# Layer 1's attention by groups of 32 queries: 176-key bands on eight parts of the array, square transposes on VectorE

## The chip, the cores and the metric

The kernel runs on one core of one Trainium2 chip. The metric is the device time of one execution in microseconds (us), the median of several. All tensors are float32 in memory; large products use two rounded halves of each operand (see below).

## The reference

A decoder trunk of two layers on 16 learned meta tokens and 256 tokens, 272 columns in all, width 2048. Layer 0 (gated linear attention, MLP) and the shared keys and values come before the place of the change; layer 1's MLP and the final norm come behind it. The change touches only layer 1's attention: 32 query heads of 64, 4 key and value heads, a sliding window of 128, the 16 meta tokens seen by all, and one learned sink per head in the softmax. Cut to that:

```python
q = rope((xn @ w_q).reshape(B, L, 32, 64), pos) * 64 ** -0.5
ok = meta (k < 16, k <= q)  or  band (k >= 16, 0 <= q - k < 128)
s = where(ok, einsum(q, keys), -1e30)
s = concatenate([s, sink])              # one column per head
p = softmax(s)[..., :-1]
o = einsum(p, vals)
h = h + o @ w_out
```

## The kernel before, in words

Activations lie transposed: 128 features on the partitions, tokens along the columns, 16 such tiles of the stream `h`. A weight comes in pieces of 128 x 1024 floats (512 KB): `fetch` (L83) issues the transfer on the SP queue into `raw` (four buffers), `split_weight` rounds it to `hi` on ScalarE (L91) and puts the rest in `lo` on VectorE (L93), three buffers each; VectorE's subtraction needs ScalarE's result. `passes` (L124 to L130) multiplies hi by x.hi, hi by x.lo, lo by x.hi: 24 matmuls for a piece of `w_q`, 256 columns each. A `product` is two pieces into one PSUM bank, after each of which it calls `after`.

Layer 1's attention runs interleaved with `w_q` and the first round of `w_out_b`. There are eight steps (class `Step`), each for four query heads: two products make its queries (`query`, four pieces, copied to `qt` at L908), and `rope` (L815 to L821) turns them into `QR`, with four copies by DMA on GpSimd's queue for the swapped halves `sw`. Behind each of the four pieces of step t there is a slot for attention work of earlier steps: in slot 0 the transposes of step t-4, in slot 2 the values of t-4 and both scores of t-2. Attention of one step is:

- `scores(0)` for 112 queries (plus 16 that are not used) against 128 keys, `scores(1)` for 128 queries against 256 keys, in PSUM banks `s` (L921);
- `soft` (L873): on VectorE, mask and sink added in and the row maximum taken, in one instruction per head, into `pr`;
- `normalise`: negated maximum (L882), exponential with row sum (L885) on ScalarE, sum and reciprocal (L887, L888) on VectorE, scaling of `pr` by the reciprocal: the 256-column part on VectorE (L891), the 128-column part on ScalarE (L893);
- `transposes` (L932): twelve 128 x 128 on TensorE, copied out by ScalarE as `PT` (L934);
- `values` (L943): six matmuls; the result is split into `O` by ScalarE (high part, L946) and VectorE (rest, L947).

The last 16 queries of all eight heads of a key head stand together in `qs` (copied by GpSimd, L912) and have their own `last_scores`, `last_transposes` and `last_values` (L953 to L980), once for every four steps. What is left of the last four steps runs behind products of `w_out_b` by the table `late`, whose keys are the product's number in round 0; each such product is one piece, and VectorE adds it to `h` at L172. PSUM has eight banks, four in pool `acc` for products and values, four in `aux`.

TensorE's order is that of the program text (`manual_schedule`); the order on the other engines is worked out by the framework's scheduler when the program is built, and each engine then takes its instructions in that order. So a wait at the head of VectorE's or ScalarE's queue holds up all behind it, `lo` and `hi` of the next pieces among them.

## Time and profile before

| | |
|---|---|
| three runs | 2042.64, 2042.83, 2045.62 us; median 2042.83 |
| the profiled execution | 2042.74 us, of which span 2041.0 |
| granted TensorE clock in it | 0.998 of full speed |
| busy in the span | TensorE 99%, VectorE 67%, ScalarE 53%, GpSimd 10% |
| layer 1's attention | about 1166 to 1310 us in the span |

In the page, PE is TensorE's matmuls, PEld its weight loads, DVE VectorE, ACT ScalarE, POOL GpSimd, SP the engine whose queue fetches the weights. A group row names source line, engine, operation, tiles (out<-in), shape and count, then busy time and the mean of one in ns, then the engine's idle time ahead of it and who ended it. Durations of neighbouring instructions overlap, since an engine is pipelined; what one costs in a row of its kind is the distance of starts, which the timeline gives. An fp32 matmul leaves two records.

### The profile page before, as it was taken

How to read it: one execution, taken by the hardware profiler on the slowest of the kernel's cores; microseconds unless marked ns; L12 is line 12 of the kernel's file. 1: busy time of each engine (PE TensorE's matmuls, PEld its weight loads, DVE VectorE, ACT ScalarE, POOL GpSimd, SP SyncE). 2: the span in 40 equal slices, each digit the busy share in tenths (PEclk: the TensorE clock that was granted, in tenths of full speed). 3: DMA queues.
4: the chain of work that ended last, by engine and by line, in shares of the span. 5: the costliest groups of instructions: out<-in, count | busy, mean ns of one | idle time of the engine just before them, and what ended most of it. 6: DMA issues, size and time to landing. Idle time of an engine off the chain costs nothing.

```text
span 2041.0 us, 39089 instructions
## 1 busy us (share of the span) xinstructions
PE 2022.1 (99%) x15978; PEld 1946.1 (95%) x15978; DVE 1374.7 (67%) x2035; ACT 1073.5 (53%) x1693; POOL 202.1 (10%) x209
## 2 busy tenths in 40 slices
PE   9999999999999999999999999999999999999997
PEld 9999999999999999999999999999999999999997
DVE  7799677665555555555566787796666666666666
ACT  6565665454345434534544577666436545545653
POOL 0000233400000000000023111160000000000032
PEclk9999999999999999999999999999999999999999
DMA  7644446565555555655554654466666666666662
GB/s 243 196 157 146 149 151 196 188 232 190 187 192 190 188 193 187 190 192 188 190 193 146 217 168 151 146 238 205 201 202 202 202 200 203 196 205 199 205 197 103
DMA packets 109124, 383.85 MB, mean 188 GB/s; under 512 B 13328, under 2 KB 15888, under 8 KB 108944
## 3 DMA queue, kind: packets, MB, share of 16 engines
q1 hardware_dynamic: 106640, 378.29, 57.5%
q8 instruction: 125, 2.05, 0.4%
q0 software_dynamic: 1152, 2.38, 0.4%
q10 hardware_dynamic: 1152, 0.68, 0.1%
q14 instruction: 55, 0.45, 0.1%
HBM read 376.82 MB, written 2.10 MB: 186 GB/s over the span
## 4 chain that ended last, share of the span: by engine, by line
PE 92%; DVE 3%; ACT 2%; issue 1%; POOL 1%; DMA 0%; SPq 0%; DVEq 0%; ACTq 0%; POOLq 0%
PE ps L124 23%; PE ps L128 18%; PE ps L130 18%; PE ps L129 18%; PE ps L125 12%; POOL sg L715 1%; DVE lo L93 1%; ACT hi L91 1%; PE ps L309 1%; PE s L921 0%; PE ps_pv L943 0%; PE pt L932 0%; ACT pr L885 0%; PE ps L311 0%; DMA raw<-in_w_in 0%
## 5 line engine op out<-in xcount | busy, mean ns | idle before, releaser
L93 DVE TENSOR_TENSOR lo<-raw,hi 128x1024 fp32r<-128x1024 f32 x707 | 871.7, 1234 | 476.4 <-ACT hi L91 470.3
L91 ACT CAST hi<-raw 128x1024 fp32r<-128x1024 f32 x707 | 738.8, 1046 | 826.2 <-PE ps L129 453.4
L130 PE MATMUL ps<-x,lo 128*128 128x272 f32 (+1 forms) x1904 | 531.8, 280 | 0.9 <-DVE lo L93 0.9
L128 PE MATMUL ps<-x,hi 128*128 128x272 f32 (+1 forms) x1904 | 531.6, 279 | 0.0
L129 PE MATMUL ps<-x,hi 128*128 128x272 f32 (+1 forms) x1904 | 531.1, 279 | 0.0
L130 PEld LDWEIGHTS ps<-x,lo 128*128 128x128 f32 x1904 | 359.9, 189 | 2.2 <-DVE lo L93 1.5
L128 PEld LDWEIGHTS ps<-x,hi 128*128 128x128 f32 x1904 | 360.2, 189 | 0.6 <-issue 0.4
L129 PEld LDWEIGHTS ps<-x,hi 128*128 128x128 f32 x1904 | 360.3, 189 | 0.1
L124 PE MATMUL ps<-x,hi 128*128 128x512 f32 x1024 | 335.7, 382 | 0.0
L124 PE MATMUL ps<-hid,hi 128*128 128x512 f32 x1008 | 330.1, 382 | 0.0
L128 PE MATMUL ps<-hid,hi 128*128 128x272 f32 (+1 forms) x1040 | 290.1, 279 | 0.0
L129 PE MATMUL ps<-hid,hi 128*128 128x272 f32 (+1 forms) x1040 | 290.1, 279 | 0.0
L130 PE MATMUL ps<-hid,lo 128*128 128x272 f32 (+1 forms) x1040 | 290.1, 279 | 0.0
L125 PE MATMUL ps<-x,lo 128*128 128x256 f32 x1024 | 279.1, 273 | 0.0
L125 PE MATMUL ps<-hid,lo 128*128 128x256 f32 x1008 | 274.1, 273 | 0.0
L124 PEld LDWEIGHTS ps<-x,hi 128*128 128x128 f32 x1024 | 193.5, 189 | 26.9
L124 PEld LDWEIGHTS ps<-hid,hi 128*128 128x128 f32 x1008 | 190.2, 189 | 26.4
L128 PEld LDWEIGHTS ps<-hid,hi 128*128 128x128 f32 x1040 | 196.6, 189 | 0.0
L125 PEld LDWEIGHTS ps<-x,lo 128*128 128x128 f32 x1024 | 196.6, 192 | 0.0
L129 PEld LDWEIGHTS ps<-hid,hi 128*128 128x128 f32 x1040 | 196.6, 189 | 0.0
L130 PEld LDWEIGHTS ps<-hid,lo 128*128 128x128 f32 x1040 | 196.6, 189 | 0.0
L125 PEld LDWEIGHTS ps<-hid,lo 128*128 128x128 f32 x1008 | 193.5, 192 | 0.2
(263 smaller groups left out, 2286.2 us busy)
## 6 DMA issues: line engine op xcount, KB each, us to landing
raw<-in_w_up SPq DMA_DIRECT2D x256, 512.0 KB, 4.3
raw<-in_w_down SPq DMA_DIRECT2D x256, 512.0 KB, 4.3
raw<-in_w_in SPq DMA_DIRECT2D x91, 512.0 KB, 3.4
raw<-in_w_out_a SPq DMA_DIRECT2D x32, 512.0 KB, 4.3
raw<-in_w_q SPq DMA_DIRECT2D x32, 512.0 KB, 4.3
raw<-in_w_out_b SPq DMA_DIRECT2D x32, 512.0 KB, 3.5
raw<-in_w_kv SPq DMA_DIRECT2D x8, 512.0 KB, 3.4
sw<-qt POOLq DMA_DIRECT2D x32, 64.0 KB, 3.5
```

Of the source, the lines that this page charges most:

```text
L91: nc.scalar.copy(hi, raw)
L93: splits.append(nc.vector.tensor_sub(lo, raw, hi.bitcast(F32)))
L124: nc.tensor.matmul(both, wh, x.both, start=begin, stop=False)
L125: newest[0] = nc.tensor.matmul(both[:, 1], wl, x.hi, start=False, stop=end)
L128: nc.tensor.matmul(out, wh, x.hi, start=begin, stop=False)
L129: nc.tensor.matmul(out, wh, x.lo, start=False, stop=False)
L130: newest[0] = nc.tensor.matmul(out, wl, x.hi, start=False, stop=end)
L309: nc.tensor.matmul(out, wk, xs[k].hi, start=False, stop=part == 1 and k == KT - 1)
L715: nc.gpsimd.tensor_scalar_max(sg, gt, -80.0)
```

## The change

The queries are now two parts of 128 (all 256 of the tokens behind the meta tokens), so the third part with `qs`, `m3`, `sinks3` and the `last_` functions is gone.

- Part 0 is scored against 144 columns (L933). Part 1 is scored in four groups of 32 queries, each against its own 176 keys: 16 meta and a band of 160 (L938). Its sixteen matmuls go round the eight 64-row by 32-column parts of the array. The bands stand in `KB`, copied once by GpSimd (L869, L870).
- `pr` holds the four heads of a part side by side with 16 columns of zeros behind each (L942), 640 or 768 columns. One instruction on VectorE transposes it in place in 32 x 32 squares (L906). No transpose of probabilities is left on TensorE, nor its copy on ScalarE.
- All scaling is on ScalarE (L904).
- `values` (L962) is 76 matmuls of 64 columns that go round the eight 32-row (some 16-row) by 64-column parts of the array and add up in four PSUM banks `pv`. The values stand for this as `VB`, 32 rows each, spread by 23 copies on the SP queue behind step 1 (L885 to L889).
- PSUM for this stage and the first round of `w_out_b`: two banks for products, two for scores, four for `pv`; afterwards four and four.
- The scores of part 0 stand in slot 0, those of part 1 in slot 2 behind the values, and `late` is new.

The diff, cut to what matters (`TILES` are the four slices of 32 partitions, `TW` is 32, `NM` 16):

```diff
+KEYS = (NM + P, 3 * NM + P)
...
+        def keys_of_blocks():
+            for g in range(1, len(TILES)):
+                nc.gpsimd.tensor_copy(KB[:, :, g - 1, :NM], KR[:, :, :NM])
+                nc.gpsimd.tensor_copy(KB[:, :, g - 1, NM:], KR[:, :, NM + g * TW:g * TW + KEYS[1]])
...
+        def spread_values():
+            for g, rows in enumerate(TILES):
+                for k, src in enumerate(TILES):
+                    nc.sync.dma_start(VB[rows, k:2 * len(TILES):len(TILES)], VT[src, :2])
+                if g:
+                    nc.sync.dma_start(VB[rows.start:rows.start + NM, NVB], VT[:NM, 0])
+                    nc.sync.dma_start(VB[rows.start + NM:rows.stop, NVB], VT[rows.start + NM:rows.stop, 0])
+            nc.sync.dma_start(VB[rows.start:rows.start + NM, NVB - 1], VT[:NM, 2])
...
-            for i, pr in enumerate(prs):
-                if pr.shape[-1] > P:
-                    nc.vector.tensor_scalar_mul(pr, pr, sm[:, i:i + 1])
-                else:
-                    nc.scalar.activation(pr, pr, AF.Copy, scale=sm[:, i:i + 1])
+            for c in range(4):
+                nc.scalar.activation(pr[:, c, :n], pr[:, c, :n], AF.Copy, scale=sm[:, c:c + 1])
+            flat = pr.rearrange("p c n -> p (c n)")
+            nc.vector.transpose(flat, flat)
...
+                    for g, rows in enumerate(TILES):
+                        for o, pp in zip(out, HALVES):
+                            keys = KB[pp, self.pair, g - 1] if g else KR[pp, self.pair, :n]
+                            nc.tensor.matmul(o[rows], self.QR[pp, i, P + g * TW:P + (g + 1) * TW], keys, start=True, stop=True)
...
             def values(self):
+                pv = pvp.tile([P, len(TILES), 512], F32, tag="pv", name="pv")
+                for part, pr in enumerate(self.probs):
+                    last = [g + 1 if part == 0 else 5 for g in range(len(TILES))]
+                    for k in range(6):
+                        for g, rows in enumerate(TILES):
+                            if k > last[g]:
+                                continue
...
+                            for par, kv in enumerate(HALVES):
...
+                                nc.tensor.matmul(dst, VB[tall, slot, self.pair, kv], src, start=k == 0, stop=k == last[g])
+                for part in range(2):
...
+                    nc.scalar.copy(oh, src)
+                    nc.vector.tensor_sub(ol, src, oh.bitcast(F32))
...
+        keys_of_blocks()
+        psum.close()
+        acc, aux, pvp = banks_of("acc2", 2), banks_of("aux2", 2), banks_of("pvp", 1)
...
+                if t >= 2:
+                    slots[0].append(partial(steps[t - 2].scores, 0))
+                    slots[2].append(partial(steps[t - 2].scores, 1))
+                if t >= 4:
+                    slots[2].insert(0, steps[t - 4].values)
...
+                if t == 1:
+                    spread_values()
...
+            late = {0: [partial(a6.scores, 0)], 2: [a4.values, partial(a6.scores, 1)], 4: [partial(a7.scores, 0)],
+                    6: [a5.values, partial(a7.scores, 1)], 9: [a6.values], 13: [a7.values]}
```

VectorE's order in one step of the steady part, before (L873 is the masking, L887 and L888 sum and reciprocal, L891 the scaling, L819 and L820 rope, L93 `lo`):

```order
L873 ISA mx 128x1
L883 TENSOR_TENSOR es<-sinks,mx 128x4
L887 TENSOR_TENSOR sm<-sm,es 128x4
L888 RECIPROCAL sm<-sm 128x4
L887 TENSOR_TENSOR sm<-sm,es 128x4
L888 RECIPROCAL sm<-sm 128x4
L891 TENSOR_SCALAR pr<-pr,sm 128x256 x4
L819 TENSOR_TENSOR QR<-qt,cos 128x512
L93 TENSOR_TENSOR lo<-raw,hi 128x1024 x3
L820 TENSOR_TENSOR sw<-sw,sin 128x2x256
```

Both parts' maskings end ahead of these rows, the two chains of sum, reciprocal and scaling follow each other, and three `lo` come in a row. After, from the end of the second part's masking (L944) to the first part's (L906 is the square transpose, L829 rope, L99 `lo`):

```order
L944 ISA mx 128x1
L897 TENSOR_TENSOR es<-sinks,mx 128x4
L901 TENSOR_TENSOR sm<-sm,es 128x4
L902 RECIPROCAL sm<-sm 128x4
L906 STREAM_TRANSPOSE pr<-pr 128x768
L99 TENSOR_TENSOR lo<-raw,hi 128x1024
L829 TENSOR_TENSOR QR<-qt,cos 128x512
L944 ISA pr,mx<-s,mask_14021,sinks 128x144
```

and from there to the second part's masking (L830 and L831 are rope, L967 the subtraction behind the values):

```order
L944 ISA mx 128x1
L99 TENSOR_TENSOR lo<-raw,hi 128x1024
L897 TENSOR_TENSOR es<-sinks,mx 128x4
L830 TENSOR_TENSOR sw<-sw,sin 128x2x256
L901 TENSOR_TENSOR sm<-sm,es 128x4
L831 TENSOR_TENSOR QR<-QR,sw 128x512
L902 RECIPROCAL sm<-sm 128x4
L99 TENSOR_TENSOR lo<-raw,hi 128x1024
L906 STREAM_TRANSPOSE pr<-pr 128x640
L99 TENSOR_TENSOR lo<-raw,hi 128x1024
L967 TENSOR_TENSOR O<-pv,O 128x4x64 x2
```

Each part's chain now stands alone between two maskings, with its square transpose ahead of a `lo`.

ScalarE's order in the same step, before (L882 negated maximum, L885 exponential, L893 scaling, L91 `hi`, L934 copy of `PT`):

```order
L882 ACTIVATE nm<-mx 128x4
L885 ACTIVATE pr,sm<-pr,nm 128x128 x4
L886 ACTIVATE es<-es 128x4
L882 ACTIVATE nm<-mx 128x4
L886 ACTIVATE es<-es 128x4
L885 ACTIVATE pr,sm<-pr,nm 128x256 x4
L893 ACTIVATE pr<-pr,sm 128x128 x4
L908 COPY qt<-ps 128x256
L91 CAST hi<-raw 128x1024 x2
L934 COPY PT<-pt 128x512 x3
L91 CAST hi<-raw 128x1024
```

and after (L896 negated maximum, L899 exponential, L904 scaling, L97 `hi`, L966 cast behind the values):

```order
L900 ACTIVATE es<-es 128x4
L899 ACTIVATE pr,sm<-pr,nm 128x176 x4
L904 ACTIVATE pr<-pr,sm 128x176 x4
L97 CAST hi<-raw 128x1024
L920 COPY qt<-ps 128x256
L97 CAST hi<-raw 128x1024
L896 ACTIVATE nm<-mx 128x4
L899 ACTIVATE pr,sm<-pr,nm 128x144 x4
L97 CAST hi<-raw 128x1024
L900 ACTIVATE es<-es 128x4
L97 CAST hi<-raw 128x1024
L904 ACTIVATE pr<-pr,sm 128x144 x4
```

The `hi` that followed the scaling of one part and stood beside the other part's work now stands behind a whole part's exponentials and scalings.

The SP queue held the 32 fetches of `w_q` in one row before. After, the 23 copies stand between the eighth and the ninth:

```order
L89 DMA raw<-in_w_q 128x1024 x8
L887 DMA VB<-VT 16x256
L885 DMA VB<-VT 32x2x256 x8
L888 DMA VB<-VT 16x256
L885 DMA VB<-VT 32x2x256 x4
L887 DMA VB<-VT 16x256
L888 DMA VB<-VT 16x256
L885 DMA VB<-VT 32x2x256 x4
L887 DMA VB<-VT 16x256
L888 DMA VB<-VT 16x256
L889 DMA VB<-VT 16x256
L89 DMA raw<-in_w_q 128x1024 x24
```

Each copy from the fourth on waits for a transfer that was issued eight before it, as the fetches do.

## The prediction

> **What bounds the kernel now.** I read the page first, then the attention stretch with the windows view, the groups by shape and the timeline. All times are us unless marked ns. Of the page, these lines:

> ```profile
> span 2041.0 us, 39089 instructions
> PE 2022.1 (99%) x15978; PEld 1946.1 (95%) x15978; DVE 1374.7 (67%) x2035; ACT 1073.5 (53%) x1693; POOL 202.1 (10%) x209
> ...
> PE 92%; DVE 3%; ACT 2%; issue 1%; POOL 1%; DMA 0%; SPq 0%; DVEq 0%; ACTq 0%; POOLq 0%
> ```

> TensorE is busy 99% of the span and carries 92% of the chain that ended last. The windows view of two stretches of layer 1's attention (columns: length, then PE, PEld, DVE, ACT and POOL busy, granted clock, DMA share, GB/s) shows how near the others are:

> ```profile
> 1192.00:1207.00 15.00, 15.00 (x137) 13.88 (x137) 14.06 (x44) 12.58 (x40) 3.37 (x5) 1.00 0.59 195
> 1237.00:1252.00 15.00, 14.71 (x136) 13.23 (x136) 11.68 (x34) 12.84 (x39) 3.26 (x5) 1.00 0.51 158
> ```

> PE has no gap to speak of, at clock 1.00. But VectorE is busy up to 14.06 of 15 us and ScalarE 12.6 to 12.8: if attention gets cheaper on PE, these two are next. The PE timeline gives the prices (start, length):

> ```profile
> 1166.63 0.28 PE L128 MATMUL ps<-x,hi 128*128 128x256 f32 x1
> ...
> 1194.05 0.28 PE L130 MATMUL ps<-x,lo 128*128 128x256 f32 x1
> 1194.17 1.47 PE L932 MATMUL pt<-ident,pr 128*128 128x128 f32 x12
> 1195.39 0.36 PE L128 MATMUL ps<-O,hi 128*128 128x256 f32 x1
> ...
> 1200.61 0.28 PE L129 MATMUL ps<-x,hi 128*128 128x256 f32 x1
> 1200.72 0.28 PE L130 MATMUL ps<-x,lo 128*128 128x256 f32 x1
> 1200.93 1.46 PE L943 MATMUL ps_pv<-PT,VT 128*64 128x224 f32 x12
> 1202.32 1.58 PE L921 MATMUL s<-KR,QR 64*128 64x128 f32 x16
> 1203.83 0.38 PE L128 MATMUL ps<-O,hi 128*128 128x256 f32 x1
> ...
> 1309.71 0.38 PE L128 MATMUL ps<-O,hi 128*128 128x256 f32 x1
> ```

> Product matmuls start 0.112 apart, so a piece (one 512 KB fetch, 24 matmuls) takes 2.68 and a step of four pieces 10.72. Transposes delay the next product matmul by 1.2 to 1.3 per step, values with both scores by 3.1 (1203.83 less 1200.72): a full step takes 15.1. From step 2's first matmul (1166.63) to the first after the last values (1309.71) lie 143.1; 24 + 14 pieces take 101.9 of it. So attention holds PE for 41.2 us. That is all the change can save there.

> **The change on PE.** Before shows nothing in 32-row parts; the nearest rows are small matmuls in column parts, early in the span:

> ```profile
> 120.44 0.38 PE L571 MATMUL ps_l<-W 128*32 128x32 f32 x18
> ...
> 141.43 0.22 PE L612 MATMUL ps_c<-QE,KD 128*64 128x64 f32 x1
> 141.44 0.22 PE L612 MATMUL ps_c<-KD,QE 128*64 128x64 f32 x1
> 141.49 0.22 PE L612 MATMUL ps_c<-QE,KD 128*64 128x64 f32 x1
> ```

> Two matmuls on different columns start 0.01 apart, the next pair (0.05 to 0.06, 0.058 over eight of them) later. Eight parts at once I take as the same, 0.058 per wave of 64 columns. Values are 76 fp32 matmuls of two records, 19 waves of one record for full eights, 22 with the uneven ends: 1.28, and 0.38 to change over when alone. First-part scores: four waves of 144 columns, 0.49 + 0.40 = 0.89. Second-part scores: four waves of 176 columns, 0.60, in one block with the values (0.55 of changeovers): 2.43. The sum is 8 x 0.89 + 2 x 1.0 + 6 x 2.43 + 2 x 1.66 = 27.0. All PE transposes and the 16-query third part are gone. If PE stayed the bound the change would win 41.2 - 27.0 = 14.2. If the eight parts ran one after another, a step's values would cost 76 x 0.058 = 4.4 instead of 1.28.
> [...]

> **The SP queue.** The 23 copies that spread the values stand between the eighth and ninth fetch of w_q. Rows of the fetches:

> ```profile
> L83 SPq DMA_DIRECT2D raw<-in_w_q x32: 327/328/335, 1132.7 to 1229.8; - x32
> ...
> DMA to landing us min/median/max: 3.1/4.3/5.9
> ```

> At 0.33 to 0.38 an issue they take 8.6; each also waits for the copy eight before it, two to three landings of 3 to 4. So the ninth fetch goes 9 to 10 us late. Four buffers of raw and those of hi and lo let a fetch lead its piece by some five pieces, 13.4; landing 4.3 and about 1.1 each for hi and lo leave 7 to 8 to spare (an estimate). PE waits 1.5 (0 to 4) at step 2.

> **VectorE and ScalarE.** Both work strictly in the order they are given, and this is what I expect to decide. Rows by shape (count, busy, mean ns, idle before), then the timeline:

> ```profile
> L93 DVE TENSOR_TENSOR lo<-raw,hi 128x1024 fp32r<-128x1024 f32 x48 | 58.3, 1223 | 16.6 <-ACT hi L91 16.4
> L172 DVE TENSOR_TENSOR h<-h,ps 128x256 f32<-128x256 f32 x16 | 6.6, 414 | 6.2 <-PE ps L130 6.2
> L820 DVE TENSOR_TENSOR sw<-sw,sin 128x512 f32<-128x512 f32 x8 | 5.5, 690 | 4.6 <-DMA sw<-qt 4.6
> L891 DVE TENSOR_SCALAR pr<-pr,sm 128x256 f32<-128x256 f32 x32 | 9.1, 350 | 0.3
> L908 ACT COPY qt<-ps 128x256 f32<-128x256 f32 x16 | 5.9, 366 | 0.0
> ```

> ```profile
> 1204.40 0.35 DVE L873 CUSTOM_DVE_ANT_0 pr<-s,m,sinks 128x128 f32<-128x128 f32 x1
> 1204.67 0.35 DVE L873 CUSTOM_DVE_ANT_0 pr<-s,m,sinks 128x128 f32<-128x128 f32 x1
> 1205.21 0.49 DVE L873 CUSTOM_DVE_ANT_0 pr<-s,m,sinks 128x256 f32<-128x256 f32 x1
> 1205.62 0.09 DVE L873 DVE_READ_ACCUMULATOR2_ANT mx<- 128x1 f32 x1
> ...
> 1209.57 0.16 DVE L887 TENSOR_TENSOR sm<-sm,es 128x4 f32<-128x4 f32 x1 [1.83 <-ACT pr L885]
> 1209.76 0.18 DVE L888 RECIPROCAL sm<-sm 128x4 f32<-128x4 f32 x1
> ```

> ```profile
> L885 ACT ACTIVATE pr<-pr,nm 128x128 f32<-128x128 f32 x32 | 12.5, 390 | 0.2
> ```

> ```profile
> 1208.46 0.49 ACT L885 ACTIVATE pr<-pr,nm 128x256 f32<-128x256 f32 x1
> 1208.95 0.49 ACT L885 ACTIVATE pr<-pr,nm 128x256 f32<-128x256 f32 x1
> ...
> 1209.44 1.26 ACT L893 ACTIVATE pr<-pr,sm 128x128 f32<-128x128 f32 x4
> 1210.61 0.35 ACT L908 COPY qt<-ps 128x256 f32<-128x256 f32 x1
> 1210.86 1.04 ACT L91 CAST hi<-raw 128x1024 fp32r<-128x1024 f32 x1
> ```

> Maskings start 0.27 apart for 128 columns and 0.41 for 256, so I take 0.285 for 144 and 0.32 for 176; exponentials 0.49 apart for 256 columns, some 0.10 less for 128 (mean 390 ns), so 0.41 and 0.43; scales (1210.61 less 1209.44, over 4) 0.29, so 0.31 and 0.33. A lo takes 1.18, a hi 0.95. For the square transpose no row exists: 0.35 for 256 columns (L891) gives 0.65 for 640 as the low end, twice lo's rate 1.5 as the high; nearest is lo's own rate, one element per step: 0.73 and 0.86.
> In before both maskings stand back to back and the exponentials of one run beside those of the other; even so VectorE waited 1.83 for the last exponential. In after each part is a chain of its own, with only one lo or none to fill it. From the second masking (S): maskings to 1.4, negated maximum and four exponentials to 3.5, sum and reciprocal 3.9, four scales 5.3, square transpose 6.2, lo, whose hi stands behind the scales, 6.35 to 7.5, cosine product 8.15. Then the first-part masking: maskings and a lo to 2.35, sw and sum 3.4, QR and reciprocal 4.3, lo to 5.5, square transpose (scales end at 5.65) 6.4, lo behind its late hi 6.7 to 7.85, then subtract, cast, subtract (0.41 like L172, 0.37 like L908), one after another because the second cast waits for the first subtraction: 9.05. Together 17.2. The last qt is copied only at S + 6.3, and its rope copies land thus:

> ```profile
> L817 POOL DMA_DIRECT2D sw<-qt x32: 536/536/553, 1157.6 to 1261.2; - x32
> ...
> DMA to landing us min/median/max: 1.8/3.8/5.9
> ```

> Four issues of 0.54 and a landing of 3.8 put sw at about S + 12.1, where VectorE asks for it at 10.65 (in before it waited 4.6 in all for these): 0 to 1.5 more, I take 0.8. The loop is then 18.0 per step, against PE's own 10.72 + 0.89 + 2.43 = 14.04, and against 15.1 before. PE would wait some 4 us in each step, at the third piece, for the lo behind the second transpose.

> **The sum.** Step 2 starts at 1168.1 (1166.63 + 1.5); two steps of 12.6 put step 4 at 1193.3 and its first masking at 1197.4. There three los, three square transposes and a wait for scales stand before the second masking: 11.6, so S is 1209.0. Four loops (17.6, the first less exposed to sw, then 3 x 18.0) and one without rope but with residual additions (16.3) give 1296.9. The lo of product 10 is done 7.4 later, and products 10 to 13 with the last values (1.66) take 12.4: 1316.7 against 1309.7. So 7 us slower: 2042.74 (this profiled run; its span 2041.0 and 1.74 around it) + 7 = 2049.7. The median of the three runs, 2042.83, is within 0.1. The rest of the kernel, two banks fewer for products in this stage aside (0 to 1 us), keeps its work. By the same sum loops of 16.6 give no change, 2043, and loops of 19 2055.

> **Rivals.**
> 1. PE stays the bound. If square transposes, exponentials and scales run faster than I take them, or the waits overlap, loops stay under 14.04 and the change wins 14.2 less the SP stall of 1.5: 2030. For it: PE carries 92% of the chain. Against it: 1.83 of waiting on one exponential already, in the looser order. Loops of 15 give about 2035. It decides where the loop passes 14.04.
> 2. Square transposes at twice lo's rate: +1.6 a loop over five loops, 2058.
> 3. The eight parts run one after another: the values cost 3.1 more per step on PE, 14.04 becomes 17.2, still under 18: the loop hides it and only the last two values show, +6: 2056.
> 4. The clock. In every row quoted it is 1.00, because PE never pauses; waits of 4 us are new. If one halves the clock for the next piece, 2.7 more lies on PE per step, of which slack takes half: some +7, 2057. [...]
> 5. The copies on SP land in time and the loop is a mere 16.6: no change, 2043. That the order is not followed by the chip is excluded: each engine's rows in the trace stand in program order.

> **How the numbers follow.** About 4.1 us (0.2%) is what a measurement of this kernel can tell from no change. Loop-bound near 2050: 0.45; loop about 16.6 and no change: 0.2; PE the bound or nearly (2030 to 2038): 0.25; transposes, parts or clock: 0.1. Slower takes 0.4 of the first and the 0.1, same 0.22, faster 0.28. The range 2033 to 2057 leaves out the lower half of the PE-bound case and the worst end; the loop's own range is 2043 to 2055.

> **What would show it.** Right: steps 4 to 7 about 18 apart, PE idle 3 to 5 us a step before a piece whose lo stands behind the 768-column transpose, VectorE idle on ScalarE's pr in each part. Wrong: PE without gaps and steps of 14; a square transpose far from 0.73 or 0.86; values far from 1.3; a stall elsewhere, as at the ninth fetch of w_q.

## The result and the profile after

The changed kernel takes 2077.56 us (median of four runs, 2077.15 to 2079.46), the kernel before 2042.74 beside it. The ratio is 1.0169, with a 95% interval of 1.0151 to 1.0187: 34.8 us slower, where 7 was forecast and 2057 was the top of the range. The sign was right, the size was not. The profiled executions stand 34.6 apart (spans 2075.6 and 2041.0).

The page of the changed kernel, its span, the engines and the chain that ended last:

```profile
span 2075.6 us, 41504 instructions
PE 2024.7 (98%) x17150; PEld 1947.5 (94%) x17150; DVE 1372.9 (66%) x2001; ACT 1069.5 (52%) x1683; POOL 200.9 (10%) x224
...
PE 84%; DVE 6%; ACT 4%; issue 2%; DMA 2%; POOL 1%; SPq 0%; DVEq 0%; ACTq 0%; POOLq 0%
```

TensorE's share of the chain falls from 92% to 84%. VectorE and ScalarE gain 5 points between them, and "DMA" and "issue", which the chain before hardly held, gain 3. Stretches of the windows view (columns as before: length, PE, PEld, DVE, ACT, POOL, clock, DMA share, GB/s):

```profile
1165.00:1180.00 15.00, 8.47 (x60) 7.99 (x60) 3.98 (x5) 3.51 (x4) 2.11 (x4) 0.77 0.72 216
1238.00:1258.50 20.50, 17.19 (x307) 15.94 (x306) 12.42 (x34) 11.81 (x36) 2.42 (x6) 1.00 0.38 107
1258.50:1277.40 18.90, 15.50 (x286) 13.77 (x284) 12.35 (x35) 11.82 (x36) 2.41 (x6) 1.00 0.42 127
```

The first is the ninth fetch of `w_q`: TensorE works 8.47 of 15 us and the mean granted clock is 0.77. The other two are one step each. PE now has gaps of some 3.4 us in each (3 to 5 were forecast), yet VectorE and ScalarE are busy only 12 of 19 to 20: no engine is full. The chain of waits in the first of those steps shows why (start, length, what; from second masking to second masking, 20.4 us):

```profile
1238.22 0.31 DVE pr L944
...
1239.94 1.71 ACT pr L899 x8
...
1242.49 1.09 ACT pr L904 x3
1243.58 0.93 ACT hi L97
1244.52 0.28 ACT qt L920
...
1245.08 1.42 POOL sw L827 x3
...
1246.66 5.47 DMA sw<-qt
...
1252.26 0.69 DVE sw L830
...
1254.18 1.02 ACT pr L904 x3
1255.20 0.94 ACT hi L97
...
1256.16 1.23 DVE lo L99
1257.39 0.34 DVE O L967
...
1258.16 0.42 DVE O L967
1258.59 0.31 DVE pr L944
```

TensorE does not occur in it. This is the loop of VectorE and ScalarE that the prediction drew, link for link, up to the subtraction of the second half of `O`. Its largest link is the landing of the rope copies, 5.47.

TensorE's own waits between 1160 and 1400 (waiting instruction, what ended the wait, total, times, longest):

```profile
PE ps L134 <- ACT qt L920: 8.1, 4, 4.5
PE ps L134 <- ACT hi L97: 6.1, 1, 6.1
PE ps L135 <- issue: 4.4, 3, 1.9
PE s L938 <- issue: 3.5, 2, 1.8
PE ps L130 <- DVE h L178: 2.5, 1, 2.5
PE pv L962 <- issue: 1.7, 1, 1.7
PE ps L136 <- DVE lo L99: 1.5, 3, 0.5
```

Four kinds: the loop (`qt`, 8.1: a product waits for one of its two banks until `qt` has been copied out), the SP queue (`hi`, 6.1), pauses that nothing in the profile releases ("issue", 9.6 in these rows), and one wait at the start of the last MLP (`h`, 2.5).

From the profiled executions the 34.6 add up so: 2.4 before step 2 (in it a gap of 1.04 that waits for a `lo`, and one of 0.90 behind the first change of PSUM pools); 8.6 at the ninth fetch; 18.5 from there to product 14; 5.1 behind it (a pause of 1.82, the MLP's gap of 2.80, and 0.5). Forecast were 0, 1.5, 5.5 and 0.

### The profile page after: what moved, and what is told of

It reads as the page before. It is cut to its first block, busy times and chain, and to the rows that moved or that the text cites. A ratio compares the mean times of both kernels' runs of the same rounds, so it can differ in the third digit from the quotient of the medians.

```text
span 2075.6 us, 41504 instructions
## 1 busy us (share of the span) xinstructions
PE 2024.7 (98%) x17150; PEld 1947.5 (94%) x17150; DVE 1372.9 (66%) x2001; ACT 1069.5 (52%) x1683; POOL 200.9 (10%) x224
## 4 chain that ended last, share of the span: by engine, by line
PE 84%; DVE 6%; ACT 4%; issue 2%; DMA 2%; POOL 1%; SPq 0%; DVEq 0%; ACTq 0%; POOLq 0%
PE ps L130 21%; PE ps L134 17%; PE ps L136 17%; PE ps L135 17%; PE ps L131 11%; DVE lo L99 2%; ACT hi L97 1%; POOL sg L721 1%; ACT pr L899 1%; ACT pr L904 1%; DMA raw<-in_w_in 1%; DMA sw<-qt 1%; DVE pr L944 1%; DVE x L189 1%; PE ps L315 0%
## 5 line engine op out<-in xcount | busy, mean ns | idle before, releaser
L99 DVE TENSOR_TENSOR lo<-raw,hi 128x1024 fp32r<-128x1024 f32 x707 | 871.5, 1233 | 483.1 <-ACT hi L97 476.7
L97 ACT CAST hi<-raw 128x1024 fp32r<-128x1024 f32 x707 | 738.4, 1045 | 828.7 <-PE ps L135 449.9
L134 PEld LDWEIGHTS ps<-x,hi 128*128 128x128 f32 x1904 | 360.9, 190 | 11.6 <-ACT hi L97 6.3
L130 PE MATMUL ps<-x,hi 128*128 128x512 f32 x1024 | 335.8, 382 | 2.5 <-DVE h L178 2.5
L130 PE MATMUL ps<-hid,hi 128*128 128x512 f32 x1008 | 330.1, 382 | 0.0
L130 PEld LDWEIGHTS ps<-x,hi 128*128 128x128 f32 x1024 | 193.5, 189 | 29.8 <-issue 2.8
L130 PEld LDWEIGHTS ps<-hid,hi 128*128 128x128 f32 x1008 | 190.2, 189 | 26.3
```

Source lines behind the costliest of these rows:

```text
L97: nc.scalar.copy(hi, raw)
L99: splits.append(nc.vector.tensor_sub(lo, raw, hi.bitcast(F32)))
L130: nc.tensor.matmul(both, wh, x.both, start=begin, stop=False)
L134: nc.tensor.matmul(out, wh, x.hi, start=begin, stop=False)
```

## The experiments

Theory A: the order loop sets the steps, as predicted, and the rest is the SP queue. Theory B: the two halves of the values and TensorE's pauses set them. Theory C, formed from the trace: four independent delays (loop, SP, code supply, change of pools) that partly cover each other. Each run has its ratio to the kernel before, timed beside it. "Steps" are the distances between second-part maskings in the three loops that the prediction put at 18.0 (the fourth to the sixth of seven); in the changed kernel they are 20.4, 18.8 and 19.3.

**1. The copies apart.** Two copies behind each piece of steps 1 to 3, instead of 23 in a row.

```diff
-                    nc.sync.dma_start(VB[rows, k:2 * len(TILES):len(TILES)], VT[src, :2])
+                    yield nc.sync.dma_start(VB[rows, k:2 * len(TILES):len(TILES)], VT[src, :2])
...
+                    for _ in range(2 if t else 0):
+                        next(spreading, None)
```

> The 23 copies that spread the values are issued two behind each piece of steps 1 to 3 instead of all behind step 1. In the changed kernel TensorE stands still from 1168.9 to 1175.3 for the ninth fetch of w_q and works the piece off until 1180.3, 8.7 us late, part of it at a granted clock of 0.77. If the SP queue did that and nothing later hides it: the pause shrinks to under 2, the clock in that stretch is 1.00, and the time falls by 6 to 8, to about 2070. If the loop of VectorE and ScalarE in steps 4 to 8 sets the end whatever comes before: no change, 2077.

2073.54 us, ratio 1.0145 (1.0129 to 1.016). The wait for `hi` goes and step 2's first scores start at 1171.57 instead of 1180.33. Of these 8.8 us only 4 reach the median. The profiled execution is the fastest of the four (2067.78; the others took 2073.25 to 2074.99) and keeps all of it: it ends 9.5 before that of the changed kernel. Where the others lose it is not shown.

**2. The values in two.** The first part's values behind the second piece, the second part's behind the third, each with its cast and subtraction.

> Values in two bursts, the first part's 28 matmuls behind the second piece of a step and the second part's 48 behind the third; same matmuls, same copies. Theory of code supply: the pauses of 1.2 to 2.1 on TensorE that nothing in the profile ends come because a burst of 76 fp32 matmuls is about 304 instructions in 1.9 us while a 16 KB packet on the instruction queue holds 256; bursts of 112 and 192 with a piece between them fit, so the pauses go and the time falls by 6 to 10, to about 2069. Theory of the order loop alone: the pauses in steps 4 to 8 are hidden in it, the time falls by at most 3 or so for the earlier cast of the first part, and pauses of about 2 stay.

2075.31, 1.0159 (1.0143 to 1.0174). The pauses named "issue" fall from 9.8 to 0.5, but a new wait takes their place, in the same banks of `pv`:

```profile
PE pv L964 <- DVE O L969: 14.4, 7, 4.0
```

The 256 instructions of the expectation are an estimate from pages of this case; the numbers stand under "Code supply" below.

**3. Both casts ahead of both subtractions.**

```diff
-                    nc.vector.tensor_sub(ol, src, oh.bitcast(F32))
+                    halves.append((ol, src, oh))
+                for ol, src, oh in halves:
+                    nc.vector.tensor_sub(ol, src, oh.bitcast(F32))
```

> Both casts behind the values first, then both subtractions, instead of cast, subtraction, cast, subtraction. Theory of the order loop: the last link ahead of the second masking gets 0.4 to 0.8 shorter in each of five loops, so the time falls by 2 to 4. Theory of code supply: nothing on TensorE changes, no change within 0.5.

2077.65, 1.017 (1.0155 to 1.0185): nothing is won in all. In the profiled execution, though, five of the seven loops are 0.1 to 0.8 shorter, and from the first second-part masking to the last it takes 121.6 instead of 123.5. But it has 27.3 us at half clock (a granted clock of 0.50) against 17.1, worth 5.1 at most. So the link was worth some 1.9, and the clock took it back.

**4. No square transposes.**

```diff
-            flat = pr.rearrange("p c n -> p (c n)")
-            nc.vector.transpose(flat, flat)
```

> Leaves out the square transposes on VectorE, so the probabilities go into the values untransposed. Theory of the order loop: 0.85 and 0.98 and the waits for the scalings ahead of them fall out of each loop; the distance of first-part maskings falls from 18 to 20 to about 16, the time by 8 to 14. Theory of code supply and of the SP queue alone: TensorE's pauses stay, the time falls by less than 2.

2076.18, 1.0171 (1.0154 to 1.0188). A miss: two transposes of 0.84 and 0.98 a step go, and the steps stay at 18.9 to 20.5. The two loops ahead of them are shorter (15.6 and 15.7 instead of 18.3 and 17.3); the last masking comes 3.6 earlier, and 1.5 of it reaches the end of the profiled execution. The `lo` behind a transpose waits for a `hi` that stands behind the same scales. The prediction's own times, 6.2 for one and 6.35 for the other, said so.

**5. Values in two bursts, both casts behind the second.**

> Values in two bursts of 28 and 48 matmuls with a piece of product between them, as in the run of two bursts before, but both casts and subtractions behind the second burst, as in the changed kernel. That run had lost its pauses without a releaser (11 us down to 0.5) and got 14.4 of waiting for the first part's subtraction in their place, because both parts share the four banks. Theory of code supply: without that wait the time falls by 8 to 12, to about 2067, and TensorE shows no pause of over 0.5 that nothing ends. Theory of the order loop: first-part maskings stay 18 to 20 apart in steps 5 to 8, and only the pauses behind the last values (some 6) are won: about 2071.

2074.39, 1.0146 (1.0131 to 1.0161). No "issue" wait is left, steps are 18.6 to 20.8. So the pauses were not what held the steps.

**6. Runs 1 and 5 together.**

> Two bursts with casts behind the second, and the 23 copies two behind each piece of steps 1 to 3. If SP queue, code supply and the half clock behind their pauses are separate costs, they add: 8.7 and 8 to 12 off, about 2057 to 2060. If the order loop of VectorE and ScalarE sets steps 5 to 8, the steps stay at 18 and the time is about 2063 to 2066.

2064.68, 1.0098 (1.0083 to 1.0113). Apart they win 4.0 and 3.2, together 12.9 (by the ratios 4.9, 4.7 and 14.5): each delay had covered part of the other. Some of it is clock: the mean granted clock is 0.995 here and 0.993 in runs 1 and 5, worth some 4.5 us at most.

**7. Run 6 without square transposes.**

> The same with the square transposes left out, so the probabilities go into the values untransposed. Theory of the order loop: now that TensorE has no pauses of its own the loop must show: first-part maskings come 1.5 to 2 closer, the time falls by 7 to 10 against the run with the squares. If VectorE's order is not what binds: the same within 2.

2062.93, 1.0091 (1.0074 to 1.0108): 1.75 less, not 7 to 10. It confirms run 4.

**8. The kernel before, with bursts of small matmuls.** 76 unused fp32 matmuls of 16 columns in steps 4 and 5, 38 in steps 6 and 7.

```diff
+                for k in range(n):
+                    kv = HALVES[k % 2]
+                    nc.tensor.matmul(pt[kv, :16], VT[0][:, 0, kv], KR[:, 0, :16], start=True, stop=True)
```

> The kernel before with a burst of unused small matmuls behind the second piece: 76 fp32 matmuls of 16 columns in steps 4 and 5, 38 in steps 6 and 7 (they go into a bank that nobody reads). Theory of code supply: each burst of 76 (304 instructions, more than a 16 KB packet of 256) shows a pause of 1.5 to 2.2 on TensorE in it or just behind it that nothing in the profile ends; the bursts of 38 (152 instructions) show none or under 0.5. Rival, that the pauses belong to the 32-row parts or to the banks: no pause with either.

A single execution: 2062.57, span 2060.9. The timeline around the first burst, and the window with it:

```profile
1199.43 5.07 PE L954 MATMUL pb<-KR,VT 128*64 128x16 f32 x152
1204.43 0.58 PE L128 MATMUL ps<-x,hi 128*128 128x256 f32 x1
```

```profile
1199.00:1210.00 11.00, 11.00 (x183) 10.62 (x183) 4.61 (x8) 4.38 (x11) 1.14 (x1) 0.70 0.46 153
```

It does not decide on code supply: on two parts the 152 records take 5.0 us (1199.43 to 1204.43), not the 1.98 of the values, so the burst is much less dense than that of the values, and no gap over 0.45 appears. Most of the 19.9 (2060.9 less 2041.0) are the bursts (5.0, 4.5 and twice 2.3) and 10.2 us at half clock, worth 5.1 at most. The granted clock fell to 0.70 in the window above without a pause; more on this below.

**9. The sum later.** Run 6, and the sum of the exponentials (L901) is ordered behind the next part's masking.

```diff
+                tc.add_manual_dep(getattr(waiting[-1], 'ins', waiting[-1]), getattr(masking, 'ins', masking).name, order, reason='order')
```

> Two bursts and copies apart as before (2064.7), and one ordering edge more per part: the sum behind the exponentials may stand on VectorE only behind the next part's masking. No instruction is added. Theory of the order loop (masking, exponentials, scales, hi, lo, masking, without TensorE): the chain of one part then runs beside the next part's, VectorE's waits of 12 us for exponentials go, first-part maskings come 16 instead of 19 apart, and the time falls by 8 to 14, to 2051 to 2057. Rival, that ScalarE's or TensorE's own work fills the steps: no change, 2064.

2062.1, 1.0088 (1.0073 to 1.0103); steps 17.6 to 18.2. VectorE's waits for exponentials go (`sm`, 12.1 in run 6). Those of the square transposes for the scales stay (12.8, now 13.2), and waits for the rope landing (4.3, now 9.1) and for `hi` (2.5, now 7.5) take their place.

**10. The square transposes later too**, behind the masking after the next.

> The same, and each square transpose behind the masking after next, so that it does not wait for the scales of its own part. Order loop: another 2 to 5 off, steps of 14.5 to 15.5, 2047 to 2053. Rival, as above: no change; or, if ScalarE's own 12 to 13 us a step now binds, no gain over the run before.

2057.96, 1.0067 (1.0051 to 1.0084); steps 17.0 to 18.5. VectorE's waits between 1190 and 1310 are now above all these:

```profile
DVE lo L99 <- ACT hi L97: 20.6, 11, 3.2
DVE sw L830 <- DMA sw<-qt: 6.5, 4, 3.0
```

**11. The two orders alone**, in the changed kernel.

> The changed kernel with the two ordering edges alone: values in one burst, copies in one block. Theory that costs of TensorE (code supply, half clock) and the order loop cover each other: the loop goes, the pauses of about 2 a step come onto the path, steps of 16 to 17, the time falls by 6 to 12, to about 2068. Rival, that the order loop alone sets steps 5 to 8: steps near 14.5, about 2060.

2071.38, 1.0133 (1.0118 to 1.0148). Steps fall to 16.7 to 18.1, but "issue" (8.8) and the stall at the ninth fetch remain. 6.2 us are won, as 6.7 were from run 6 to run 10.

**12. The rope product later.** Run 10, and `sw` times `sin` (L830) behind the next step's second masking.

> The kernel of e10_squares_later (copies apart, values in two bursts, exponential sums and square transposes behind the next masking), and the multiplication sw by sin (L830) is put behind the second masking of the next step as well, so that the second masking no longer stands behind the landing of the rope copies. In e10 VectorE waited 10.2 us in all for these landings. Theory (the order loop passes through the rope landing): steps fall from 17.0-18.6 to 15.5-16.5, the time from 2058 to 2049-2052. Rival A (the loop is held by ScalarE alone: hi behind exponentials and scales): the wait moves to lo<-hi, steps stay at 17-18, 2055-2058. Rival B (half-clock stretches hold the time): no change.

2051.24, 1.0038 (1.0024 to 1.0052), steps 16.9 to 18.0. Two steps of it:

```profile
1214.90:1231.80 16.90, 16.19 (x330) 14.71 (x329) 11.87 (x34) 11.74 (x36) 2.41 (x7) 1.00 0.48 143
1231.80:1248.70 16.90, 14.92 (x304) 13.96 (x294) 11.87 (x34) 11.74 (x36) 2.41 (x7) 1.00 0.48 143
```

6.7 us less: the rope landing was a link of the loop. Up to 3 us of it may be clock (on average 0.995 was granted in run 10, 0.997 here). With the link gone most steps are equal, 16.9, and VectorE waits mainly for `hi` (25.2 between 1190 and 1310, in 20 waits).

**13. Run 12 without scales.** The probabilities stay undivided.

```diff
-            for c in range(4):
-                nc.scalar.activation(pr[:, c, :n], pr[:, c, :n], AF.Copy, scale=sm[:, c:c + 1])
```

> As e12_swaps_later, but the four scales of every part are left out (the probabilities stay without their division by the sum). ScalarE loses eight instructions of 0.29 to 0.33 a step, 2.5 us. If ScalarE's queue is what holds the steps behind the edges, they fall by 2 to 2.5 more, to TensorE's own 14 to 15, and the time by 8 to 12 against e12, to 2040-2046. If the chain from exponentials to sum does not pass ScalarE's scales, 0 to -3.

2041.5, 0.9988 (0.9978 to 0.9998). A step:

```profile
1216.40:1231.30 14.90, 14.90 (x291) 13.98 (x290) 11.89 (x35) 9.28 (x28) 2.44 (x7) 1.00 0.59 163
```

TensorE is full, at 14.9 a step (with the values in two bursts) and clock 1.00. So ScalarE's scales were what the loop still had over TensorE's own work.

**14. The kernel before with the pools changed**, closed and opened at the two places, four banks each.

```diff
+        psum.close()
+        acc, aux = banks_of("acc2", 4), banks_of("aux2", 4)
...
+        psum.close()
+        acc, aux = banks_of("acc3", 4), banks_of("aux3", 4)
```

> The kernel before, with its two PSUM pools closed and opened again at the two places where the changed kernel does it (ahead of step 0 of layer 1's attention, and ahead of the last MLP), four banks each as before: nothing else changes. If it is the change of pools that cost the changed kernel 2.4 at the start and 2.8 at the MLP, this costs +3 to +6, 2046-2049, and the gaps stand at the same places (bank waits on kv products' readers at about 1131 to 1146, and on the residual's h at about 1360 to 1390). If it is only the fewer banks of the stage (two for products), no change: 2043 plus or minus 1.

2047.84, 1.0018 (1.0009 to 1.0028). In the kernel before, PE waited for none of these; here:

```profile
PE ps L128 <- DVE h L176: 2.4, 1, 2.4
PE ps L132 <- DVE vt L854: 0.6, 1, 0.6
```

They are gaps of 2.67 and 0.90, as in the changed kernel (2.80 and 0.90).

**15. The banks the other way round.** Run 12, with the values' pool opened first, and at the MLP the auxiliary pool.

```diff
-        acc, aux, pvp = banks_of("acc2", 2), banks_of("aux2", 2), banks_of("pvp", 1)
+        pvp, acc, aux = banks_of("pvp", 1), banks_of("acc2", 2), banks_of("aux2", 2)
...
-        acc, aux = banks_of("acc3", 4), banks_of("aux3", 4)
+        aux, acc = banks_of("aux3", 4), banks_of("acc3", 4)
```

> The kernel of e12_swaps_later with the order of the new PSUM pools turned round: the pool of the values opens first (on the banks of the kv products), the products' pool after it; at the MLP the four other banks first. The first product behind each change then writes banks that were read out long before. If the gaps at the changes (0.90 at 1145.5 and 2.79 at 1361.3 in e12; 0.90 and 2.67 in e14) are waits for the last readers of those very banks, they go: -3 to -4, 2047-2048. If a change of pools waits for all banks of the old pools, they stay: 2051.

2055.51, 1.0061 (1.0046 to 1.0076): 4.3 more than run 12, not less. The first gap (0.90) goes. The second stays at 2.79, because my two swaps together put the MLP's products back on the banks of the last products. The steps are those of run 12; the profiled runs differ by 13.7 us at half clock against 3.4.

**16 and 17. The first part's scales on VectorE, or on GpSimd**, on top of run 15.

```diff
+                if n == KEYS[0]:
+                    nc.gpsimd.tensor_scalar_mul(pr[:, c, :n], pr[:, c, :n], sm[:, c:c + 1])
+                else:
```

> As e15_pools_swapped, and the four scales of the first part (128x144) go from ScalarE to VectorE. In e12 a step of 16.9 has VectorE busy 11.87 and ScalarE 11.74; the chain goes from one to the other. ScalarE loses 1.33 a step, VectorE gains some 1.0. If the chain of handovers binds, the hi behind the scales comes about 1.3 earlier and the step is some 1 shorter: 16, five steps, 2042-2044 from 2047.5. If the sum of both engines' work along the chain is what counts, only 0.3 a step: 2046.

> As e15_pools_swapped, and the four scales of the first part go to GpSimd, which is busy 2.4 of 16.9 us in a step. If they take 0.3 to 0.6 each there, the hi is free of them as in e16 and VectorE carries nothing more: steps 15 to 16, 2041-2045. If they take 1 us and more, the square transpose of the first part is late and the steps lengthen: 2050 and more.

2044.95, 1.001 (1.0001 to 1.002), steps 15.4 to 15.5; and 2044.41, 1.0007 (0.9998 to 1.0017), steps 15.6 to 15.8. GpSimd takes 881 ns for what ScalarE does in 402 and VectorE in 291, and still a step is some 1.2 shorter than in run 15:

```profile
L918 POOL TENSOR_SCALAR pr<-pr,sm 128x144 f32<-128x144 f32 x32 | 27.8, 881 | 51.7 <-DVE sm L915 34.9 <-ACT pr L912 16.8
```

What counted here is whose queue the `hi` stands in, not how fast the scales are. Neither profiled execution has a half-clock stretch in the stage, where run 15 has 10.2 us of it, so up to 5.1 of the 11 us won are clock.

**18. Run 17 with the products' pool first at the MLP again**, so that its products stand on the values' banks.

> As e17_scales_pool, but at the MLP the pool of the products opens first again, as in the changed kernel. In e15 and e17 both orders were turned, so that the MLP's products came to stand on the very banks of the last products again, and the gap of 2.79 stayed. Now they stand on the banks of the values, read out long before. If the gap is a wait for the readers of those banks, it goes: -2 to -3, 2041.5-2042.5, the same as before. If a change of pools waits for every bank of the old pools, it stays: 2044.4.

2040.82, ratio 0.9985 (0.9976 to 0.9994). The gap at the MLP is gone and the time falls by 3.6 us: it had been a wait for those very banks. This version is 3 us faster than the kernel before, with an interval that just leaves out 1.

## Why the prediction was right in sign and wrong in size

The profiled executions stand 34.6 apart, 27.6 more than the 7.0 forecast. Of these, 2.4 lie ahead of step 2, 7.1 at the ninth fetch, 2.4 between it and the first loop, 4.6 in the five loops, 6.0 behind the last masking and 5.1 from product 14 on. So the forecast failed in two steps of its sum: the SP term, priced from the wrong row (1.5, measured 8.6), and the terms put at nothing: TensorE's pauses, the half clock beside the loop, and the change of pools. The loop, on which it spent most of its work, came out 4.6 short.

**TensorE's side: right.** The timeline has one step's values, the groups by shape have the two square transposes (count, busy, mean ns, idle before):

```profile
1229.84 1.98 PE L962 MATMUL pv<-pr,VB 32*64 32x64 f32 x152
```

```profile
L906 DVE STREAM_TRANSPOSE pr<-pr 128x768 f32<-128x768 f32 x8 | 7.8, 978 | 8.6 <-ACT pr L904 8.5
L906 DVE STREAM_TRANSPOSE pr<-pr 128x640 f32<-128x640 f32 x8 | 6.7, 843 | 2.9 <-ACT pr L904 2.7 <-ACT O L966 0.2
```

Values were put at 1.66 with their changeover, the transposes at 0.86 and 0.73: near enough. The eight parts do run side by side: 152 records in 1.98 are 13 ns each. Run 13 gives TensorE's own step as 14.9, where the sum had 14.04, and before it was 15.1: there was less to win than the 14.2 that were put for eight steps and the tail. Rivals 2, 3 and 5 (slow transposes, parts one after another, a loop of 16.6) fall; rival 1 (TensorE stays the bound) falls for the order as it stands, and comes true once the loop is cut (run 13).

**The loop: right mechanism, one link too short.** Forecast 18.0, measured 18.8 to 20.4. The link is the rope landing: `qt` was copied at S + 6.3 (forecast 6.3), but in the longest loop `sw` began at S + 14.0 (1252.26 less 1238.22), not 12.1. The landing was taken as its median, 3.8; there it took 5.47, inside the 1.8 to 5.9 that the row gave. In the other two, of 18.8 and 19.3, `sw` began at S + 12.6 and 12.8, and counting 0.8 of the 1.45 by which it came too late was too little as well. Five loops, up to the masking at 1313.4, came to 92.5 against 87.9, 4.6 more. Runs 9, 10 and 12 took the loop apart edge by edge (2.6, 4.1, 6.7 us) and run 13 took out the rest of it. Removing work from it that is not its last arrival (runs 3, 4, 7) won 1.75 us at most. PE's wait was forecast at the `lo` behind the second transpose; it stood instead at the product's bank, which waits for `qt`.

**The SP queue: a price from the wrong row.** Forecast 1.5 (0 to 4), measured 8.6. The issue of a copy was taken at 0.33 to 0.38 from the row of the 512 KB fetches. The copies' own row and the fetch behind them (start, busy):

```profile
L885 SPq DMA_DIRECT2D VB<-VT x16: 594/596/1035, 1155.1 to 1167.2; - x16
```

```profile
1154.42 0.61 SPq L887 DMA_DIRECT2D VB<-VT  x1
...
1169.77 2.04 SPq L89 DMA_DIRECT2D raw<-in_w_q  x4
```

23 copies took 15.35 (1169.77 less 1154.42), 0.67 each, not 8.6. The 6.7 more are nearly the whole miss of this term, for the 7 to 8 us that could be spared were already used up. The prediction had named a stall at this fetch as a sign of being wrong, and run 1 takes it out.

**Code supply: no term at all.** Six pauses that nothing releases (1.24 to 2.13, 11.3 us in all) each begin 0.1 to 1.0 us behind the start of a packet on the instruction queue, whose packets are all of 16384 bytes in this trace (20 of them start between 1160 and 1345). The one at 1231.93, whose packet started at 1231.65, and the page's row of the queue (packets, MB):

```profile
1231.93 0.34 PE L938 MATMUL s<-KB,QR 64*32 64x176 f32 x5
1233.99 0.33 PE L938 MATMUL s<-KB,QR 64*32 64x176 f32 x1 [1.73 <-issue]
```

```profile
q8 instruction: 134, 2.20, 0.4%
```

If the queue carries TensorE's instructions and little else, which was not shown, 2.20 MB for 2 x 17150 records (as many matmuls as weight loads) give an estimated 64 bytes for each, and 16384 by 64 some 256 to a packet; the page of before, with 125 packets of 2.05 MB in all and 2 x 15978 records, gives 64 too. A burst of 76 fp32 matmuls is 304 instructions (152 records of each kind) in 1.98 us. With bursts of 112 and 192 instructions the "issue" waits of TensorE came to 0.5 in run 2 and to none in run 5. Where no slack is left a pause shows in full. From the last second-part masking (1313.4) to product 14 it took 25.8 instead of 19.8. The forecast had four pieces and one step's values there, behind a `lo`. But TensorE, which had paused for 2.13 within the last scores, still had seven pieces (18.8) and two steps' values (4.0) to do from 1313.0 on, paused for 2.13 once more, and lost 1.3 to the half clock. In the kernel before, 18 such packets start between 1120 and 1400, and no two matmuls start more than 0.56 apart there. That the packets cause the six pauses is inferred from their times and from runs 2 and 5; run 8 was meant to show it directly and could not, so this cause stays open.

**The clock: rival 4, in part.** TensorE had half clock (0.50 granted) in 1172.13 to 1178.96, 1281.36 to 1288.19 and 1312.08 to 1315.49, 17.1 us, worth 8.5 at most. Gaps of 6.34, 4.74 and 2.13 stand ahead of them; the last section has more of what stood there. That a wait in each step halves the clock for the next piece, as rival 4 had it, was not shown: from 1178.96 to 1281.36 the granted clock was 1.00, though gaps of up to 2.04 lie in it. The forecast's 7 us for it was not far off, but it came beside the loop, not instead of it.

**The change of pools: no term.** The 0 to 1 us of the prediction were for two banks fewer for products. Run 14 has the change alone: 3.7 (interval 1.8 to 5.7). The gap of 1.04 ahead of step 2 is not of this kind: run 14 does not have it, run 18 still does, and its cause stays open.

**The range.** It was built from the loop and from TensorE. The other delays were each put at nothing or at the small end, though all of them could only lengthen, and each came from something that the trace of before does not have. The sign came out because the loop, the SP queue and all that was left out lengthen alike; it says little for the sum.

## What to carry to other kernels

When work moves off a full engine, draw the order loop of the engines that take it, and put the slowest plausible landing, not the median, on every DMA in it: what stands behind that landing in a strictly ordered queue waits too. Then ask of each instruction in the loop not how long it is but what stands behind it: moving a sum, a transpose and a rope product past the next masking, and four scales to a slower engine, won 20 us (run 6 to run 17, the clock and the order of the pools included), while leaving out the transposes won 2. Small copies put into a queue of large fetches, bursts of some hundreds of TensorE instructions in 2 us (304 in 1.98 here, with pauses whose cause stays open), and a pool that is opened again on banks just read each want a term of their own.

## What the runs showed of the hardware

So a gap here cost itself, or itself and up to 1.7 (an estimate: 3.41 us at a granted 0.50). The MLP's gap of 2.8 shows both. In run 15 it goes from 1364.17 to 1366.96, one window holds 2.71 of it, and the granted clock of the next is 0.50 (a window and the next, columns as before):

```profile
1364.25:1367.66 3.41, 0.89 (x6) 0.68 (x5) 3.38 (x5) 2.01 (x3) 3.05 (x3) 1.00 0.64 210
1367.66:1371.08 3.42, 3.42 (x13) 2.96 (x12) 1.47 (x3) 0.41 (x1) 1.55 (x2) 0.50 1.01 405
```

In the changed kernel it goes from 1388.35 to 1391.15, the fuller window holds 2.24 of it, and the granted clock stays at 1.00:

```profile
1387.17:1390.59 3.42, 1.45 (x10) 1.07 (x8) 3.35 (x7) 1.50 (x3) 2.97 (x4) 1.00 0.44 161
1390.59:1394.00 3.41, 2.85 (x17) 2.67 (x18) 2.37 (x4) 1.04 (x3) 2.55 (x3) 1.00 0.94 323
```

This fits the several us by which executions of one kernel spread here (2067.78 to 2074.99 in run 1), and the 4.3 that run 15 lost against run 12 with the same steps (13.7 us at half clock against 3.4 in the profiled runs); that it is their cause was not shown.
